# Eight gate tiles moved into the up projection, weights loaded a load ahead at the start, and a written ScalarE order at the end

## The chip, the cores and the metric

One core of a Trainium2 chip runs the whole kernel. Its engines work beside each other, each through its own list of instructions in order: TensorE (PE) multiplies, VectorE (DVE) and ScalarE (ACT) work element by element, GpSimd (POOL) issues some transfers, SyncE (SP) issues most of them. An instruction that waits holds up all that stand behind it on its engine, and a transfer issued from ScalarE stands in ScalarE's list. The metric is the device time of one execution in microseconds: 2152.03 us before, the median of three runs (2150.7 to 2157.48).

## The reference

One layer of a diffusion block over 512 latent tokens and 256 context tokens, width 2048, in float32:

```python
mod_l = (silu(c) @ w_ada + b_ada)          # 6 x 2048 values: sh_a sc_a gt_a sh_f sc_f gt_f
mod_c = (silu(c_ctx) @ w_ada + b_ada)      # the same for the context
h_l = modulate(rms_norm(x, g_mix_norm), sh_a, sc_a)
h_c = modulate(rms_norm(ctx, g_mix_norm), csh_a, csc_a)
...  = split_projection(h_l @ w_in)        # attention of 8 heads, and a gated short convolution
x = x + gt_a * merge_heads(att_l, conv_l, g_mix_out, w_out)
hf_l = modulate(rms_norm(x, g_ffn_norm), sh_f, sc_f)
x = x + gt_f * conv_ffn(hf_l, w_up, ffn_conv_w, ffn_conv_b, w_down)
return rms_norm(x, g_final)
```

## The kernel before

The tokens lie along the free dimension, 512 columns; the width is cut into 16 tiles of 128 rows. Every float32 operand is split into a high part, which ScalarE casts (names that end in h), and a low part, which VectorE subtracts (names that end in l), and a product is three matmuls (`mm3`): high by high, high by low, low by high. So every weight tile needs a transfer, a cast and a subtraction before TensorE can use it.

The work goes through stages, one after the other. **Start**: c and c_ctx are spread over the partitions by matmuls with a row of ones and pass through silu (`silu_rows`, L405 and L406) into sv and svc; the 16 tiles of x are squared on ScalarE and added up on VectorE into one total (`add_squares`, L346, L347), whose column sums (`rms_steps`, L308), square root and reciprocal (`rsqrt`, L281, L283) give the factor rl (L319). **Input projection**: 31 output tiles, the 16 tiles of the width taken in three chunks of 2, 4 and 10. In a chunk the first G = 6 outputs (banks pf) take the tiles as they get ready; then the others follow (banks pp). A tile gets ready by `prep`: its shift and scale are dots of two rows of w_ada with sv on VectorE (two of 128x1024 a tile, L233), then x * rl (L427), scale and shift on ScalarE (L430), and the split into h0h, h0l and so on. Weights are loaded where they are used (`load`, names rf, rw). In the chunk's end `evac` copies a bank on ScalarE (chunk 0, L531) or adds it on VectorE. **Attention**, **output projection**, and in these the late w_ada tiles 32 to 87, two dots of 128x1024 each (`late_dot`, L255). In the last two outputs of the output projection the residual (L955), its squares, the second norm and the modulated tiles hf0, hf1, ... follow each other, and the **up projection** starts on them with the weights ufw0, ufw1, ... (`split4`, L998, L999). From f = 3 on it works by a Strassen-like scheme, seven products of eight triples of matmuls for each f (`product`; p1, p2, p6, q5, p7, and for the f before, q4 and q3), each with a cast of 128x1024 on ScalarE and a subtraction on VectorE. The last eight tiles of w_ada, 88 to 95, are dotted in the **down projection** in quarters of 128x512 (aq, L1249), which works by products of seven triples (v0 to v23; `seven`, `into`). **End**: the two last steps v22 and v23 run interleaved; the final norm is made for each half of the tokens, and the outputs, scaled ahead by g_final on ScalarE (`scale_out`, L1416), are multiplied by the norm's factor (`final`, L1409) and stored.

A planner orders each engine's instructions by its own estimate of durations, except where the code fixes the order: `keep` holds instructions of one engine in the order in which they are written, and `issue_after` puts one behind another. Tiles come from pools: a tile with one buffer can be loaded anew only when its last reader is done.

## Time and profile before

| | us |
|---|---|
| median of three runs | 2152.03 |
| profiled execution | 2158.83 |
| its span, first to last instruction | 2157.0 |
| TensorE busy | 2104.9 |
| VectorE busy | 1769.0 |
| ScalarE busy | 1047.1 |
| first matmul of the input projection | 29.62 |
| first matmul of the up projection | 815.16 |

A line of a timeline has the start and duration of an instruction, its engine and line, what it writes and reads, how many like it follow, and in brackets the time that the engine was idle before it and what it waited for. Where an engine is late the brackets name its releaser, and the releaser's own row tells why that was late. The mean granted clock of TensorE is 0.994 of full speed.

### The profile page before, as it was taken

The page shows a single profiled execution, that of the slowest core. Times are in us where ns is not written, and L with a number is a line of the kernel's source. Part 1 is how long each engine was busy: PE and PEld are TensorE (multiplying, and loading weights), DVE is VectorE, ACT ScalarE, POOL GpSimd, SP SyncE. Part 2 cuts the span into 40 slices and gives each one's busy share as a digit, 9 for nine tenths or more (in the row PEclk, how much of TensorE's full clock was granted, in tenths as well). Part 3 has the DMA queues.
Part 4 walks back from the last instruction along what each step waited for, and adds up shares of the span by engine and source line. Part 5 has one row for each costly group of instructions (what it writes and reads, how often), then busy time and mean ns, then how long its engine had stood idle before and what let it go on. Part 6 is the DMA issues. An engine that isn't in the chain of part 4 may idle for free.

```text
span 2157.0 us, 37744 instructions
## 1 busy us (share of the span) xinstructions
PE 2104.9 (98%) x14458; PEld 1946.7 (90%) x14458; DVE 1769.0 (82%) x2859; ACT 1047.1 (49%) x1710; POOL 188.1 (9%) x270
## 2 busy tenths in 40 slices
PE   7899999999999999999999999999999999999997
PEld 4688788888888888999999999999999889999997
DVE  7998987778886889788888788788888658888877
ACT  5533333555552237555555555555555333333445
POOL 0000000000000000111211111111111000000000
PEclk9999999999999999999999999999999999999998
DMA  9979785334559986577887877877887999877683
GB/s 335 345 275 337 270 279 176 128 126 162 177 199 348 344 278 192 159 217 201 241 232 215 240 229 220 237 231 219 241 229 218 341 335 290 254 220 236 196 247 111
DMA packets 162121, 513.89 MB, mean 238 GB/s; under 512 B 18962, under 2 KB 23314, under 8 KB 156306
## 3 DMA queue, kind: packets, MB, share of 16 engines
q1 hardware_dynamic: 133364, 418.14, 56.5%
q0 software_dynamic: 27488, 92.29, 18.3%
q8 instruction: 113, 1.85, 0.3%
q10 hardware_dynamic: 1088, 1.05, 0.1%
q14 instruction: 68, 0.56, 0.1%
HBM read 464.22 MB, written 46.14 MB: 237 GB/s over the span
## 4 chain that ended last, share of the span: by engine, by line
PE 86%; DVE 6%; DMA 5%; issue 1%; ACT 1%; SPq 0%; DVEq 0%; POOLq 0%; ACTq 0%
PE pp L187 4%; PE pp L189 4%; PE pp L188 4%; PE o L189 1%; PE o L187 1%; PE o L188 1%; DMA ada<-in_w_ada 1%; PE d L187 1%; PE d L189 1%; PE d L188 1%; PE uf L187 1%; PE uf L188 1%; PE of L187 1%; PE of L188 1%; PE of L189 1%
## 5 line engine op out<-in xcount | busy, mean ns | idle before, releaser
L1044 POOL DMA_DIRECT2D t_d<-tp x126 | 71.9, 574 | 468.3 <-DVE tp L1043 465.4
L255 DVE SCALAR_TENSOR_TENSOR ada<-ada,sv 128x1024 f32<-128x1024 f32 x68 | 82.1, 1219 | 12.1 <-DMA ada<-in_w_ada 12.0
L166 ACT CAST w_0h<-rw 128x512 fp32r<-128x512 f32 (+1 forms) x63 | 38.3, 618 | 108.3 <-PE pp L188 63.1
L1121 POOL DMA_DIRECT2D u_s<-in_w_up x80 | 70.2, 878 | 224.4 <-DMA u_s<-in_w_up 131.5
L233 DVE SCALAR_TENSOR_TENSOR ada<-ada,sv 128x1024 f32<-128x1024 f32 x64 | 77.5, 1217 | 4.4 <-DMA ada<-in_w_ada 3.9
L522 DVE SCALAR_TENSOR_TENSOR ada<-ada,svc 128x1024 f32<-128x1024 f32 x64 | 76.0, 1220 | 2.3 <-DMA ada<-in_w_ada 2.3
L785 POOL TENSOR_TENSOR gr<-gr,half 128x8 f32<-128x8 f32 x4 | 10.1, 2524 | 628.7 <-DVE gr L784 536.8
L1042 ACT CAST tp<-a 128x256 fp32r<-128x256 f32 x90 | 34.7, 405 | 60.5 <-DMA t_d<-tp 54.1
L167 DVE TENSOR_TENSOR w_0l<-rw,w_0h 128x512 fp32r<-128x512 f32 (+1 forms) x63 | 42.6, 681 | 22.3 <-ACT w_0h L166 22.3
L255 DVE SCALAR_TENSOR_TENSOR ra<-ra,sv 128x1024 f32<-128x1024 f32 x44 | 52.5, 1217 | 1.1 <-DMA ra<-in_w_ada 1.1
L1213 DVE TENSOR_TENSOR u<-u,u_s 128x1024 f32<-128x1024 f32 x40 | 48.8, 1219 | 0.7 <-DMA u_s<-in_w_up 0.7
L1214 DVE TENSOR_TENSOR u<-u,u 128x1024 f32<-128x1024 f32 x40 | 48.7, 1218 | 0.0
L1043 DVE TENSOR_TENSOR tp<-a,tp 128x256 fp32r<-128x256 f32 x90 | 36.2, 418 | 12.3 <-ACT tp L1042 12.3
L756 ACT CAST pth<-t 128x384 fp32r<-128x384 f32 x64 | 28.6, 485 | 26.4 <-PE t L753 26.4
L1042 ACT CAST tp<-ts 128x256 fp32r<-128x256 f32 x36 | 14.6, 407 | 43.5 <-DMA t_d<-tp 41.1
L533 DVE TENSOR_TENSOR acc<-acc,pp 128x512 f32<-128x512 f32 x50 | 34.0, 680 | 2.1 <-PE pp L189 2.1
L757 DVE TENSOR_TENSOR ptl<-t,pth 128x384 fp32r<-128x384 f32 x64 | 33.2, 549 | 2.7 <-ACT pth L756 2.7
L737 DVE TENSOR_REDUCE mn<-s 128x1 f32<-128x768 f32 x32 | 30.4, 952 | 4.8 <-PE s L726 4.6
L1043 DVE TENSOR_TENSOR tp<-ts,tp 128x256 fp32r<-128x256 f32 x36 | 15.2, 421 | 23.3 <-ACT tp L1042 23.3
L1005 ACT ACTIVATE g<-cg,sm 128x512 f32<-128x512 f32 x40 | 32.5, 813 | 0.5 <-DVE cg L1182 0.5
L1005 ACT ACTIVATE a<-ca,sm 128x512 f32<-128x512 f32 x40 | 32.1, 803 | 0.0
L1013 ACT ACTIVATE g<-g 128x512 f32<-128x512 f32 x43 | 27.2, 632 | 6.4 <-DVE g L1007 6.4
(15967 smaller groups left out, 9398.2 us busy)
## 6 DMA issues: line engine op xcount, KB each, us to landing
ada<-in_w_ada SPq DMA_DIRECT2D x196, 512.0 KB, 6.0
u<-in_w_up SPq DMA_DIRECT2D x120, 512.0 KB, 8.2
w<-t_d SPq DMA_DIRECT2D x161, 256.0 KB, 5.2
u_s<-in_w_up SPq DMA_DIRECT2D x80, 512.0 KB, 4.3
u_s<-in_w_up POOLq DMA_DIRECT2D x80, 512.0 KB, 8.9
t_d<-tp POOLq DMA_DIRECT2D x126, 256.0 KB, 4.9
v<-in_w_dnw SPq DMA_DIRECT2D x72, 384.0 KB, 5.4
ra<-in_w_ada SPq DMA_DIRECT2D x22, 1024.0 KB, 4.9
```

What stands on the lines that cost most here:

```text
L187: PE.matmul(ps, w[0], x[0], start=first, stop=False, skip_group_check=on_top)
L188: PE.matmul(ps, w[0], x[1], start=False, stop=False, skip_group_check=on_top)
L189: PE.matmul(ps, w[1], x[0], start=False, stop=last, skip_group_check=on_top)
L233: V.scalar_tensor_tensor(out=r, in0=r, scalar=1.0, in1=vec[:, i * 1024:(i + 1) * 1024], op0=ALU.mult, op1=ALU.mult, accum_out=col[:, i:i + 1])
L255: keep(V.scalar_tensor_tensor(out=r, in0=r, scalar=1.0, in1=svs[i], op0=ALU.mult, op1=ALU.mult, accum_out=lc[:, t % 4:t % 4 + 1] if i else ...
L522: keep(V.scalar_tensor_tensor(out=raw[q], in0=raw[q], scalar=1.0, in1=svc[:, q * 1024:(q + 1) * 1024], op0=ALU.mult, op1=ALU.mult, accum_o ...
L1005: A.activation(u, src, AF.Identity, bias=s("fb", m), scale=s("fw", 86 + m))
L1042: A.copy(out=z[:, :256], in_=src)
L1043: V.tensor_tensor(out=z[:, 256:], in0=src, in1=z[:, :256].bitcast(F32), op=ALU.subtract)
L1044: G_.dma_start(t_d[p, OPS.index(n)], z.bitcast(F32))
L1121: G_.dma_start(r[-1], src[more], accum_op=ALU.add)
L1213: V.tensor_tensor(out=a11, in0=a11, in1=s1, op=ALU.add)
```

## The change

There are three edits, at the start, from the output projection to the up projection, and at the end.

**Start.** The squares are added into two totals of eight tiles, and both are given to the column sums. c_ctx is no longer spread by matmuls: after chunk 1's first banks it is loaded to all partitions at once, with one silu over 128x2048. The dots of tiles 16 and 0 get places of their own around the reciprocal (`first_scale`, `prep_first`). The input projection's weights are loaded one load ahead (`load_next`, `weights`), and for a while casts and subtractions of weights are put behind the last cast or subtraction of a tile.

**Gate tiles.** The late tiles end at 80. Tiles 80 to 87 are dotted in the up projection, in 32 quarters of 128x512, one transfer from ScalarE each and all in one buffer (tag ts, which `pair_sums` uses too), and four loads of a quarter of sv into rl. A product can issue a quarter or dot the one that is under way, where no background work stands.

**End.** In the last two steps ScalarE's casts, squares and scalings keep the order in which they are written, the scalings of outputs are spread over the products, the weights of the last four products are split early (`apart`), the factor is read from PSUM, and two of the stores of the second half go out from ScalarE instead of four.

```diff
-    late = {"t": 32, "raw": None, "end": 88}
+    late = {"t": 32, "raw": None, "end": 80}
...
-        recips[:] = [V.reciprocal(r, r)]
+        with tc.issue_after(ahead.pop()) if ahead else ExitStack():
+            recips[:] = [V.reciprocal(r, r)]
...
+        def first_scale():
+
+            first["raw"] = [ada_load(t) for t in (16, 0)]
+            first["col"] = [tiny(2, f"dv{t}") for t in (16, 0)]
+            for i in range(2):
+                first["last"] = first_dot(0, i)
+            total(first["col"][0], 16, mod[:, 16:17])
...
+        def prep_first():
+
+            a = first_dot(1, 0, recips[0].ins)
+            with tc.issue_after(a):
+                b = V.tensor_tensor(out=xs[0], in0=xs[0], in1=rl, op=ALU.mult).ins
+            first_dot(1, 1, b)
+            low_after[:] = [total(first["col"][1], 0, mod[:, 0:1]).ins]
...
-            ssq = add_squares(ssq, xs[j], T, f"xs{j}")
-        silu_rows(c_ctx, svc, "cc")
+            ssq = add_squares(ssq if j % 8 else None, xs[j], T, f"xs{j}")
+            if j % 8 == 7:
+                sqs.append(ssq)
         fetch_to(sm, small)
-        rms([ssq], D, T, rl)
+        first_scale()
+        ahead.append(first["last"])
+        rms(sqs, D, T, rl)
...
+        def load_next():
+            if loads:
+                a, k = loads.popleft()
+                ready.append(load(w_in[:, a:a + k], k, f"rw{a}"))
+
+        def weights(ahead=True):
+
+            raw = ready.popleft()
+            if ahead:
+                load_next()
+            return raw
...
-                    prep(q)
+                    prep(q) if q else prep_first()
+                    if q:
+                        load_next()
...
             if ci == 1:
+
+                fetch_to(svc, c_ctx.to_broadcast([P, D]))
+                A.activation(svc, svc, AF.Silu)
...
-                    k = min(per, len(ORDER) - G - i) * n
-                    raw = load(w_in[:, off:off + k * P], k * P, f"rw{ci}_{m}")
-                    off += k * P
+                    raw = weights()
...
+    def gate_mods():
+
+        if way:
+            r, q, i, n = way.pop()
+            if n < 3 and not bg:
+                way.append((r, q, i, n + 1))
+                return
+            V.scalar_tensor_tensor(out=r, in0=r, scalar=1.0, in1=rl, op0=ALU.mult, op1=ALU.mult, accum_out=lu[:, i, q:q + 1])
...
+        elif quarters and not bg:
+            q, i = quarters.popleft()
+            if i == 0:
+                A.dma_start(rl, sv_d[:, q * T:(q + 1) * T])
+            r = cp.tile([P, T], F32, tag="ts", bufs=1, name=f"au{i}{q}")
+            A.dma_start(r, w_ada[80 + i][:, q * T:(q + 1) * T])
+            way.append((r, q, i, 0))
+
     def product(ps, a, n, nm, first):
...
+        gate_mods()
         pump(1)
...
+    def apart(a, nm):
+
+        r = []
+        for c in range(0, WIN * P, T):
+            k = min(T, WIN * P - c)
+            hi, lo = (t2([P, T], F32R, f"{nm}{c}{x}") for x in "hl")
+            keep(A.copy(out=hi[:, :k], in_=a[:, c:c + k]))
...
-            (A if h and j % 4 else SP).dma_start(out[j:j + 2, :, HS[h]].rearrange("a p t -> p a t"), o)
+            (A if h and j % 4 and j > 8 else SP).dma_start(out[j:j + 2, :, HS[h]].rearrange("a p t -> p a t"), o)
...
     d_p6(za)
+    scale(0, [0])
     d_q3(prev)
     ended(prev)
     d_p6(zb)
+    scale(0, [2, 4])
     for z in (za, zb):
         squares(z.m, H0)
     d_p7(za)
+    scale(0, [6, 8])
     d_p7(zb)
+    scale(0, [10])
+    scale(1, [0])
     d_q4(za)
+    za.s1 = apart(za.s1, "xa5")
+    scale(1, [2])
+    d_q4(zb)
     sqs = [ssq, add_squares(None, acc2[za.m + 1][:, H0], T // 2, "eqa", a=0)]
-    scaled = {j: scale_out(j, 0) for j in range(0, za.m, 2)}
-    d_q4(zb)
+    keep(opened[-1])
+    zb.s1 = apart(zb.s1, "xb5")
+    za.a12 = apart(za.a12, "xa3")
+    zb.a12 = apart(zb.a12, "xb3")
+
+    keep(A.activation(tiny(1, "root"), eps, AF.Sqrt))
     sqs.append(add_squares(None, acc2[zb.m + 1][:, H0], T // 2, "eqb", a=0))
...
```

On SP's queue, at the weights of the first chunk (rw is a load of w_in, ada a half of a row tile of w_ada), the order before was:

```order
L145 DMA rw_13_337<-in_w_in 128x2048
L145 DMA ada_360<-in_w_ada 128x1024
L145 DMA ada_362<-in_w_ada 128x1024
L145 DMA ada_368<-in_w_ada 128x1024
L145 DMA ada_370<-in_w_ada 128x1024
L145 DMA ada_449<-in_w_ada 128x1024
L145 DMA ada_451<-in_w_ada 128x1024
L145 DMA ada_457<-in_w_ada 128x1024
L145 DMA ada_459<-in_w_ada 128x1024
L145 DMA rw_21_473<-in_w_in 128x2048
```

and is now:

```order
L145 DMA ada_284<-in_w_ada 128x1024
L145 DMA rw_298<-in_w_in 128x2048
L145 DMA rw_330<-in_w_in 128x2048
L145 DMA ada_353<-in_w_ada 128x1024
L145 DMA ada_355<-in_w_ada 128x1024
L145 DMA ada_361<-in_w_ada 128x1024
L145 DMA ada_363<-in_w_ada 128x1024
L145 DMA ada_442<-in_w_ada 128x1024
```

The load rw_21_473, now rw_330, has moved to right behind the load before it.

On ScalarE, at the end of the first part of the up projection and the first Strassen-like product (T and hf are casts of the operands, ufw and u3p of weights), the order before was:

```order
L998 CAST ufw14h<-ufr_8286 128x768
L1085 CAST T23h<-x_7165 128x256
L1085 CAST T43h<-x_7165 128x256
L941 CAST hf15h<-x_7267 128x512
L998 CAST ufw15h<-ufr_8348 128x768
L1085 CAST hf12h<-x_7071 128x256
L998 CAST u3p1h<-u_11_8242 128x1024
L1085 CAST T23h<-x_7267 128x256
L1085 CAST T43h<-x_7267 128x256
L998 CAST u3p2h<-u_12_8244 128x1024
```

and is now, with au for the quarters of w_ada:

```order
L1266 DMA au_8689<-in_w_ada 128x512
L1163 CAST T23h<-x_7155 128x256
L1163 CAST T43h<-x_7155 128x256
L1073 CAST ufw15h<-ufr_8289 128x768
L1163 CAST hf12h<-x_7065 128x256
L1266 DMA au_8949<-in_w_ada 128x512
L1012 CAST hf15h<-x_7239 128x512
L1266 DMA au_9103<-in_w_ada 128x512
L1163 CAST T23h<-x_7239 128x256
L1073 CAST u3p1h<-u_11_8183 128x1024
L1163 CAST T43h<-x_7239 128x256
L1266 DMA au_9347<-in_w_ada 128x512
```

Four of the first eight quarter loads have come between the casts, each of which waits for VectorE's dot of the one before.

On ScalarE, around the cast v23p6h in the last two steps (out is a scaled output, eq a square for the final norm, both of sums c), the order before was:

```order
L1416 ACTIVATE out_23626<-c_19120,sm 128x256
L1416 ACTIVATE out_23626<-c_19122,sm 128x256
L1416 ACTIVATE out_23629<-c_19124,sm 128x256
L1416 ACTIVATE out_23629<-c_19126,sm 128x256
L1416 ACTIVATE out_23728<-c_18797,sm 128x256
L1416 ACTIVATE out_23728<-c_18799,sm 128x256
L1416 ACTIVATE out_23731<-c_18801,sm 128x256
L1416 ACTIVATE out_23731<-c_18803,sm 128x256
L1416 ACTIVATE out_23734<-c_18805,sm 128x256
L1416 ACTIVATE out_23734<-c_18807,sm 128x256
L1416 ACTIVATE out_23737<-c_18809,sm 128x256
L998 CAST v23p6h<-v_23322 128x768
```

and is now:

```order
L1073 CAST v21q3h<-v_22974 128x768
L359 ACTIVATE eq_23555<-c_19168 128x512
L359 ACTIVATE eq_23558<-c_19170 128x512
L1073 CAST v23p6h<-v_23366 128x768
L1534 ACTIVATE out_23584<-c_18845,sm 128x256
L1534 ACTIVATE out_23584<-c_18847,sm 128x256
L1534 ACTIVATE out_23587<-c_18849,sm 128x256
L1534 ACTIVATE out_23587<-c_18851,sm 128x256
L359 ACTIVATE eq_23590<-c_19172 128x256
L359 ACTIVATE eq_23593<-c_19176 128x256
L1073 CAST v22p7h<-v22s_23172 128x768
```

The eleven scalings ahead of v23p6h have gone, and two squares have come there; scalings follow behind it.

## Rows read from the trace of the kernel before

**Rows 1.** The page, busy time of each engine, share and instructions

```profile
PE 2104.9 (98%) x14458; PEld 1946.7 (90%) x14458; DVE 1769.0 (82%) x2859; ACT 1047.1 (49%) x1710; POOL 188.1 (9%) x270
```

**Rows 2.** Stretches: busy us (instructions) by engine, granted clock, DMA share, GB/s

```profile
30.00:100.00 70.00, 60.98 (x246) 46.34 (x246) 62.72 (x126) 38.10 (x70) 0.00 (x0) 1.00 0.92 340
862.00:900.00 38.00, 38.00 (x228) 33.74 (x227) 29.14 (x46) 20.74 (x33) 2.83 (x4) 1.00 0.52 139
900.00:1650.00 750.00, 750.00 (x6252) 750.00 (x6252) 621.63 (x823) 429.95 (x644) 133.96 (x199) 1.00 0.80 226
815.00:820.00 5.00, 4.83 (x29) 4.84 (x30) 5.00 (x13) 4.96 (x13) 0.00 (x0) 0.67 1.01 397
```

**Rows 3.** TensorE's waits: us in total, times, longest

```profile
PE pp L187 <- ACT acc L531: 7.2, 6, 2.0
```

**Rows 4.** Timeline at the start: start, us, engine, instruction, [idle before <- releaser]

```profile
22.75 1.87 PE L308 MATMUL rs<-io,xs0t 128*128 128x1 f32 x8
29.62 2.07 PE L187 MATMUL pf<-h0h,wf_0h 128*128 128x512 f32 x4 [3.21 <-ACT h0h L329]
...
18.80 0.69 DVE L347 TENSOR_TENSOR xs0t<-xs0t,xs 128x512 f32<-128x512 f32 x1
19.41 1.22 DVE L233 SCALAR_TENSOR_TENSOR ada<-ada,sv 128x1024 f32<-128x1024 f32 x1
...
25.06 0.18 DVE L283 RECIPROCAL rr<-rr 128x4 f32<-128x4 f32 x1 [0.41 <-ACT rr L281]
```

**Rows 5.** Timeline in the first chunk, ScalarE and TensorE

```profile
53.31 0.62 ACT L166 CAST w_0h<-rw 128x512 fp32r<-128x512 f32 x1 [6.04 <-DMA rw<-in_w_in]
...
54.46 0.50 PE L187 MATMUL pp<-h0h,w_0h 128*128 128x512 f32 x1 [1.98 <-ACT acc L531]
...
57.73 0.50 PE L187 MATMUL pp<-h0h,w_0h 128*128 128x512 f32 x1 [1.62 <-ACT acc L531]
```

**Rows 6.** Timeline at the step into the up projection

```profile
814.28 0.83 ACT L998 CAST ufw0h<-ufr 128x768 fp32r<-128x768 f32 x1
...
809.73 0.28 PE L189 MATMUL ol<-mx15h,o151w1536l 128*128 128x256 f32 x1
...
815.16 0.58 PE L187 MATMUL uf<-hf0h,ufw0h 128*128 128x256 f32 x1 [0.88 <-ACT ufw0h L998]
```

**Rows 7.** Line L1249 by groups; landing of aq's loads, then of rq's

```profile
L1249 DVE SCALAR_TENSOR_TENSOR aq<-aq,svq 128x512 f32<-128x512 f32 x32 | 21.2, 687 | 7.7 <-DMA aq<-in_w_ada 6.1 <-DMA svq<-sv_d 1.7
...
DMA to landing us min/median/max: 3.0/6.0/8.3
...
DMA to landing us min/median/max: 2.5/2.7/3.4
```

**Rows 8.** Tiles u14p6l and u3p6l: xcount, ns min/median/max, first and last start

```profile
L189 PE MATMUL u14a<-T20h,u14p6l x2: 285/285/285, 1112.2 to 1112.6; 128*128 128x256 f32 x2
...
L999 DVE TENSOR_TENSOR u14p6l<-u,u14p6h x1: 1226/1226/1226, 1107.4 to 1107.4; 128x1024 fp32r<-128x1024 f32 x1
...
L189 PE MATMUL u3a<-T20h,u3p6l x2: 284/284/284, 890.7 to 891.1; 128*128 128x256 f32 x2
```

**Rows 9.** Timeline at the end: ScalarE, VectorE, TensorE

```profile
2115.25 4.50 ACT L1416 ACTIVATE out<-c,sm 128x256 f32<-128x256 f32 x11
2119.66 0.82 ACT L998 CAST v23p6h<-v 128x768 fp32r<-128x768 f32 x1
...
2128.11 1.28 ACT L1467 ACT_TABLE_LOAD   x1
2129.40 0.20 ACT L1467 ACTIVATE root<-eps 128x1 f32<-128x1 f32 x1
...
2118.90 0.48 DVE L1338 SCALAR_TENSOR_TENSOR c<-v21c,mod,c 128x256 f32<-128x256 f32 x1 [1.65 <-PE v21c L189]
...
2120.53 0.38 PE L187 MATMUL v23a<-w,v23p6h 128*128 128x256 f32 x1 [1.67 <-ACT v23p6h L998]
...
2137.08 0.50 PE L308 MATMUL rs<-io,eqbt 128*128 128x1 f32 x4
```

More of the change, by code (lines that the diff above doesn't have):

```diff
@@ L426, in modulate @@
             xr = xs[j]
[L427 removed]
+            if j:
+                keep(V.tensor_tensor(out=xr, in0=xr, in1=rl, op=ALU.mult))
             sc = tiny(1, f"sc{j}")
@@ L554, in block_kernel @@
         todo[1, 22] = [(prep, 13)]
-        off = 0
+        loads, off = deque(), 0
+        for n in KCH:
+            per = max(1, 2048 // (n * P))
+            for k in [2 * G] * (n // 2) + [min(per, len(ORDER) - G - i) * n for i in range(0, len(ORDER) - G, per)]:
+                loads.append((off, k * P))
+                off += k * P
+        ready = deque()
+        def load_next():
[8 more added lines that the diff above has]
+        load_next()
         for ci, (k0, n) in enumerate(zip(K0, KCH)):
@@ L1228, in block_kernel @@
     finish(pend)
+    assert not quarters and not way
     phc.close()
@@ L1444, in block_kernel, with scale @@
     za, zb = nxt, weights_of(STEPS - 1)
+    written[0] = True
+    scaled = {}, {}
+    def scale(h, js):
+        for j in js:
+            scaled[h][j] = scale_out(j, h)
     d_p1(za)
@@ L1456, in block_kernel, with factor @@
     d_p7(za)
+    scale(0, [6, 8])
     d_p7(zb)
+    scale(0, [10])
+    scale(1, [0])
     d_q4(za)
+    za.s1 = apart(za.s1, "xa5")
+    scale(1, [2])
+    d_q4(zb)
     sqs = [ssq, add_squares(None, acc2[za.m + 1][:, H0], T // 2, "eqa", a=0)]
[L1460 to L1467 removed]
+    keep(opened[-1])
[3 more added lines that the diff above has]
+    keep(A.activation(tiny(1, "root"), eps, AF.Sqrt))
+    sqs.append(add_squares(None, acc2[zb.m + 1][:, H0], T // 2, "eqb", a=0))
+    fac = []
+    def factor(steps):
+        for r in steps:
+            fac.append(r)
+            yield
+    bg.append(factor(rms_steps(sqs, D, 0, T // 2, None, wait=1, one=True, hold=True)))
+    outs = final(0, fac, scaled[0])
     pump(1)
@@ L1470, in block_kernel @@
     squares(za.m + 1, H1)
-    d_q5(zb, (1,), lambda: [keep(next(outs)) for _ in range(2)])
+    d_q5(zb, (0,), lambda: [keep(next(outs)) for _ in range(2)])
     keep(last_into[0])
+    scale(0, [12, 14])
     squares(zb.m + 1, H1)
-    scaled = {j: scale_out(j, 1) for j in range(0, za.m, 2)}
     keep(next(outs))
@@ L1490, in block_kernel @@
         keep(ins)
-    for ins in final(1, r, scaled):
+    scale(1, [8, 10, 12, 14])
+    for ins in final(1, r, scaled[1]):
         keep(ins)
```

78 lines of the change are left out of this document (56 added, 22 removed).

## The prediction

> **What bounds the kernel now.** I read the busy times first. The reader is to see that TensorE is busy for 2104.9 of 2157.0 us [rows 1], so at most about 52 us can be had without taking matmuls away, and the change takes none. Next came the table by stretches: where TensorE is busy all the time, as in nearly the whole up projection [rows 2] (third row), nothing is to be won, and something can be lost. Between 30 and 100 us it is idle for 70.00 − 60.98 = 9.02 us [rows 2] (first row). Then I read TensorE's waits [rows 3] and, at each place that the change touches, the timeline of the engines that TensorE waits for: the start [rows 4, 5], the step into the up projection [rows 6] and the end [rows 9]. The profiled execution took 2158.83 us, 1.83 us of it outside its span, and the median of the runs shown is 2152.03 us; I sum changes of the span and take them off the median.
>
> **The start.** Before, TensorE runs the eight matmuls that spread c and c_ctx until 22.75 and only then sums the squares [rows 4]. The c_ctx half, and the four ScalarE steps behind it, leave the start. In the changed order the last square's addition is one fewer (0.69 us off DVE's chain, which ended at 18.80 + 0.69 = 19.5), so the sums can run from 18.7, in 1.87 us, to 20.6; the table load (1.28 us, as in [rows 9]) fits in while ScalarE waits, and the square root is ready near 20.9. Two dots of 1.22 us stand on DVE before the reciprocal, 18.7 to 21.0, so the reciprocal comes near 21.1 (25.06 before). From there the old chain has 29.62 − 25.06 = 4.56 us to the first matmul; the new one has a second dot behind the multiply (1.22 us) but no weight lows ahead of it, and I put it at 5.5 us: first matmul 26.6, **−3.0 us**.
>
> **The first chunk.** Two of the six waits for the copy out of a bank, 1.98 and 1.62 us [rows 5], have one cause: ScalarE, in its order, stood 6.04 us at a cast for a weight load and the copies stood behind it. That load (rw_21 before, rw_330 now) stands right behind the load before it on SP's queue, ahead of the eight ada loads that stood between, so I take both away: **−3.6**. The four other waits make 7.2 − 3.6 = 3.6 us [rows 3]. They come from ScalarE's in-order wait for VectorE at xr, and VectorE is some 3 to 4 us earlier now; I take half, **−1.8** (bounds 0 and −3.6). Against it: the three matmuls that filled the wait for h1h now stand behind it, 3 x 0.25 us (60.98 us for 246 matmuls, the first row of [rows 2]), **+0.7**; and the weight loads now go ahead of ada loads for which VectorE waits. Their cost the trace does not show; it is between 0 and the 3.6 us that comes free, and I take **+1.5**. Context's silu moves behind chunk 1's first banks: one load, one long activation and a table load on ScalarE, where no row of TensorE's waits stands between 90 and 200 us, and two casts are made ahead of it, which hide it; uncovered it would cost its table load, 1.3 us, and about 2 us of activation. I take 0. Start and first chunk: −3.0 − 3.6 − 1.8 + 0.7 + 1.5 = **−6.2** (−10 to −3).
>
> **The step into the up projection.** VectorE has the dots of the last late tiles between the residuals there; the first matmul of the up projection starts 815.16 − 810.0 = 5.2 us after the last of the output projection [rows 6]. With eight tiles gone, no dot stands there. The last residual can follow the last matmul at about 810.3; behind it on ScalarE now stand one square, one scaled tile and the cast ufw0h, of which the cast is the longest with 0.83 us; I put the three at 1.8 us, so the first matmul comes near 812.1: **−3.0**. Behind the gap the granted clock was 0.67, between its two levels of 1.2 and 2.4 GHz (0.5 and 1), for 4.83 busy us [rows 2] (fourth row), which cost about 1.6 us; if a shorter gap spares that, it is −4.6; the other end is −2.
>
> **The price in the up projection.** The 16 dots of 1.22 us become 32 of 0.69 us [rows 7], 22 us of VectorE, each with its own load of 256 KB. All go through one buffer: each load waits, on ScalarE's queue, for the dot before it, and the casts queued behind it wait as well. Eight stand close together at the start, two in each odd f after that, 12 such pairs. Where landing takes as long as the same size took at its best-served place, 2.7 us median, the casts and lows of u3 come in time by my count and TensorE loses nothing; at 6.0, the median of the later gate's loads [rows 7], the eighth link of the chain brings u3p6l by my count at 896.2 against 890.7 where it is wanted [rows 8]: 5.5 us. Between them the cost begins at about 3.2 us of landing. The DMA engines are half busy in that stretch, 0.52 [rows 2] (second row), so I lean to the first row: **+1.5** (0 to 5.5). In the pairs, VectorE's lows are done 1112.2 − 1108.6 = 3.6 us before TensorE wants them [rows 8], and a pair's second load is issued about 3.0 us before its dot: a landing up to 6.6 us costs nothing, so I take 0 there. The Trainium skill ("DMA: Bandwidth & Descriptors", Anatomy of one DMA) gives about 2 us and the bytes at 436 GB/s, by which 256 KB would be an estimated 2.6 us; the 2.7 row agrees, the 6.0 row does not, and by the page the sum would be 1.5 us lower. The same page (Issuing engines are not separate DMA queues) speaks against the change: a load from ScalarE's queue shares the 16 engines with the up projection's stream; by that the 6.0 row is nearer, and the sum would be 4.0 us higher. Which of the two holds no row tells, since nothing was loaded from ScalarE's queue there.
>
> **The end.** Before, TensorE waits 1.67 us at v23p6h, because eleven output scalings stood before that cast on ScalarE (2115.25 to 2119.66) [rows 9]. The change takes them away from there but writes two squares ahead of the cast, and these need the sum that VectorE makes at 2118.90 to 2119.38. So: squares at 2119.42 and 2119.95, cast 2120.47 to 2121.30, first matmul 2121.3 instead of 2120.53: **+0.8**. The early weight pieces for the last four products cost ScalarE and VectorE work that lies beside matmuls. Six short casts, the table load and the root then stand before the square eqbt, on which the first half's sum waits: 2138.4 by my count against 2137.08 [rows 9], of which 0.8 is counted; **+0.5**. The outputs behind the second reciprocal remain eight of 0.6 us, and the stores behind them the same bytes: 0. The end: **+1.3** (−1 to +3). In the trace the table load took 1.28 us and the root began 1.29 us after its start [rows 9]. The Trainium skill ("ScalarE: Activation LUTs", What ACT_TABLE_LOAD costs) adds a drain of about 1.38 us to each load; the row shows none, and by the page the end would be 1.4 us later still.
>
> **Sum.** −6.2 − 3.0 + 1.5 + 1.3 = −6.4 us: a span of 2150.6, a profiled execution of 2152.4, and against the median 2152.03 − 6.4 = **2145.6 us**. What a measurement can tell from no change is 0.3%, 6.5 us, so my value lies on that border.
>
> **Rivals.**
> (1) All stalls go: the first chunk's other half (−1.8), no contention there (−1.5), no price in the up projection (−1.5), and no slow clock after the shorter gap (−1.6): −6.4 − 6.4 = −12.8, 2139.2 us. For it: VectorE is idle for 7 us between 30 and 100 and is the last cause of most waits. Against: the DMA engines are full there (0.92) [rows 2], so something arrives late.
> (2) The chain of eight loads becomes the wait that ends last: 5.5 in place of 1.5, −2.4, 2149.6 us. For it: the same loads' median of 6.0; against: DMA engines half idle in that stretch, and 2.7 us for the same size elsewhere [rows 7].
> (3) Slower: the second load of each pair decides. VectorE stands in order at that dot with u..p6l behind it. At 8.3 us, the longest of the same loads [rows 7], it stands 8.3 − 3.0 = 5.3 us, 1.7 more than the 3.6 us of cover; 12 pairs cost 20 us, with (2) 20 − 2.4 = +17.6, 2169.6 us; at 7.6 us it is 1.0 a pair, 12 − 2.4 = +9.6, 2161.6 us. It decides from a landing of 6.6 us up. For it: the DMA engines carry the weights and the products' stores all through that stage, 0.80 busy [rows 2]. Against: the dots can fall behind and catch up, for VectorE is busy for only 621.63 of 750 us there [rows 2].
> (4) The change does not do what it says at the end: if the two squares are not what ScalarE stands at, the 1.67 us wait goes and the end is −1.2 instead of +1.3: 2143.1 us, inside the main case.
>
> **How the numbers follow.** Main case, with (4), 0.48: 2142 to 2149. Rival (1) 0.20: 2138 to 2142. Rival (2) 0.20: 2148 to 2151. Rival (3) 0.12: 2154 to 2170. The range from 2138 to 2154 leaves out (3) and a little below. Faster means under 2145.6: just over half of the main case and all of (1), 0.46. Slower means over 2158.5: most of (3), 0.10. Within: 0.44.
>
> **What would show it.** Right: the first pf matmul near 26.6, no wait for the copies near 54 and 58, the first uf matmul 2 to 2.5 us after the last residual's matmul, au loads landing in 3 us or less at the start of the up projection, TensorE busy without a gap through all its pairs, and a wait of over 2 us at v23p6h. Wrong: gaps of 1 us and more repeated at the p6 products (rival 3), a gap of some 5 us at u3 or u4 (rival 2), VectorE waiting for ada loads in the first chunk longer than before, or a v23p6h that starts before 2120 less the time won.

## The result, and the profile after

The changed kernel takes 2161.42 us, the median of nine executions (2151.39 to 2166.44); the kernel before, run beside it, takes 2151.78 (2148.32 to 2157.71). The ratio is 1.0039, with a 95% interval of 1.0023 to 1.0055. It is slower, with an interval that stays clear of 1. The forecast was 2145.6 us with a range to 2154: wrong in sign and out of range.

The profiled execution of the change took 2151.39 us, 10 below its own median, while that of before, 2158.83, lies 7 above its. A comparison of those two spans alone would show a gain of 7.4 us that the medians turn round. So stages are compared below, and with more than one execution.

The busy time of the engines, from the page of the change, answers to [rows 1]:

```profile
PE 2090.8 (97%) x14458; PEld 1935.2 (90%) x14458; DVE 1766.0 (82%) x2893; ACT 1047.4 (49%) x1712; POOL 188.1 (9%) x270
```

The same stretches as in [rows 2], the second moved 7 us and the last to its place behind the step: stretch, length, busy us (instructions) of PE, PEld, DVE, ACT, POOL, granted clock, DMA share, GB/s.

```profile
30.00:100.00 70.00, 63.28 (x255) 48.99 (x254) 60.41 (x121) 40.33 (x70) 0.00 (x0) 0.98 0.91 336
855.00:893.00 38.00, 36.50 (x214) 31.90 (x214) 30.32 (x54) 19.52 (x31) 2.26 (x3) 1.00 0.62 168
900.00:1650.00 750.00, 744.56 (x6246) 742.09 (x6245) 631.16 (x873) 427.16 (x642) 134.80 (x200) 1.00 0.82 236
808.00:815.00 7.00, 6.70 (x57) 6.70 (x57) 6.58 (x13) 5.41 (x13) 0.00 (x0) 1.00 0.94 325
```

The third row is the one that matters: where TensorE was busy for 750.00 of 750 us [rows 2], it now has holes. The fourth row has a clock of 1.00 where it was 0.67. The first has 0.98 where it was 1.00; what that is follows below.

The start, TensorE and VectorE, answers to [rows 4]:

```profile
18.67 1.87 PE L316 MATMUL rs<-io,xs8t 128*128 128x1 f32 x8 [4.01 <-DVE xs8t L360]
26.87 2.07 PE L193 MATMUL pf<-h0h,wf_0h 128*128 128x512 f32 x4 [4.64 <-ACT h0h L337]
...
20.88 0.18 DVE L291 RECIPROCAL rr<-rr 128x4 f32<-128x4 f32 x1
22.88 0.69 DVE L448 TENSOR_TENSOR xr<-xr,rl 128x512 f32<-128x512 f32 x1 [0.50 <-ACT rl L327]
```

In the first chunk TensorE still waits five times for a copy out of a bank. These are three of the five in its timeline, and the cast on ScalarE ahead of the longest; they answer to [rows 5]:

```profile
55.43 0.50 PE L193 MATMUL pp<-h0h,w_0h 128*128 128x512 f32 x1 [0.96 <-ACT acc L571]
...
68.83 0.50 PE L193 MATMUL pp<-h0h,w_0h 128*128 128x512 f32 x1 [0.95 <-ACT acc L571]
72.56 0.55 PE L193 MATMUL pp<-h0h,w_0h 128*128 128x512 f32 x1 [2.08 <-ACT acc L571]
...
71.40 0.62 ACT L167 CAST wf_0h<-rw 128x512 fp32r<-128x512 f32 x1 [1.39 <-DMA rw<-in_w_in]
```

TensorE at the step into the up projection, against [rows 6]: 2.7 us from the last matmul of the output projection to the first uf, where it was 5.2.

```profile
805.35 0.28 PE L195 MATMUL ol<-mx15h,o151w1536l 128*128 128x256 f32 x1
807.35 0.61 PE L316 MATMUL rs<-io,fq0t 128*128 128x1 f32 x4 [1.72 <-DVE fq0t L360]
808.30 0.39 PE L193 MATMUL uf<-hf0h,ufw0h 128*128 128x256 f32 x1 [0.34 <-ACT ufw0h L1073]
```

TensorE's waits between 870 and 1670 us (in all, times, longest), three of eight, which make 6.8 us. Before, it had none there.

```profile
PE u22b L195 <- DVE u22p2l L1077: 1.6, 1, 1.6
PE u25a L195 <- DVE u25p6l L1077: 1.1, 1, 1.1
PE u3a L195 <- DVE u3p6l L1077: 1.0, 1, 1.0
```

To see why u22p2l is late, follow the timeline back, TensorE first, then VectorE and ScalarE:

```profile
1257.85 0.39 PE L195 MATMUL u22b<-hf1h,u22p2l 128*128 128x256 f32 x1 [1.56 <-DVE u22p2l L1077]
...
1254.83 1.23 DVE L1318 TENSOR_TENSOR u<-u,u_s 128x1024 f32<-128x1024 f32 x1 [3.46 <-DMA u_s<-in_w_up]
1256.58 1.22 DVE L1077 TENSOR_TENSOR u22p2l<-u,u22p2h 128x1024 fp32r<-128x1024 f32 x1
...
1266.10 0.41 ACT L1120 CAST tp<-ts 128x256 fp32r<-128x256 f32 x1 [4.26 <-DMA t_d<-tp]
1275.86 0.41 ACT L1120 CAST tp<-a 128x256 fp32r<-128x256 f32 x1 [3.55 <-DMA t_d<-tp]
```

VectorE's low u22p2l stands behind a sum of weights (u) that waited 3.46 us for u_s, which SyncE loads and GpSimd then adds to. GpSimd issues the stores t_d too, and a cast tp waits for such a store to free its buffer; the two casts shown stand behind u22p2l and ahead of the next late low, u23p2l. In all, VectorE and ScalarE wait so in the change, from their waits:

```profile
DVE au L1255 <- DMA au<-in_w_ada: 21.1, 21, 2.3
DVE u L1318 <- DMA u_s<-in_w_up: 16.7, 11, 3.5
...
ACT tp L1120 <- DMA t_d<-tp: 145.9, 68, 4.6
```

and ScalarE before:

```profile
ACT tp L1042 <- DMA t_d<-tp: 93.0, 61, 2.9
```

The second row of the change has no counterpart among VectorE's waits of before. The quarters' loads landed after (shortest, median, longest; first all 32, then the 24 in pairs behind 900 us), to be held against [rows 7]:

```profile
DMA to landing us min/median/max: 3.0/4.9/10.2
...
DMA to landing us min/median/max: 3.4/8.4/10.2
```

The median of all hides two groups. Of each pair the first load, issued late in an even f, landed after 8.4 to 10.2 us, the second, in the odd f behind it, after 3.4 to 4.9 (where the trace has the landing).

The end, ScalarE, then TensorE, answers to [rows 9]:

```profile
2110.11 1.15 ACT L359 ACTIVATE eq<-c 128x512 f32<-128x512 f32 x2 [5.97 <-DVE c L1455]
2111.16 0.82 ACT L1073 CAST v23p6h<-v 128x768 fp32r<-128x768 f32 x1
...
2127.47 1.28 ACT L1598 ACT_TABLE_LOAD   x1
2128.76 0.20 ACT L1598 ACTIVATE root<-eps 128x1 f32<-128x1 f32 x1
...
2112.03 0.39 PE L193 MATMUL v23a<-w,v23p6h 128*128 128x256 f32 x1 [2.48 <-ACT v23p6h L1073]
```

The squares eq stand 5.97 us for VectorE's sum c, and the cast behind them makes TensorE wait 2.48 us, where it was 1.67.

### The profile page after: what moved, and what is told of

Its sections match the earlier page's. It is cut to its first block, busy times and chain, and to the rows that moved or that the text cites. A ratio compares the mean times of both kernels' runs of the same rounds, so it can differ in the third digit from the quotient of the medians.

```text
span 2149.6 us, 37791 instructions
## 1 busy us (share of the span) xinstructions
PE 2090.8 (97%) x14458; PEld 1935.2 (90%) x14458; DVE 1766.0 (82%) x2893; ACT 1047.4 (49%) x1712; POOL 188.1 (9%) x270
## 5 line engine op out<-in xcount | busy, mean ns | idle before, releaser
L240 DVE SCALAR_TENSOR_TENSOR ada<-ada,sv 128x1024 f32<-128x1024 f32 x60 | 72.8, 1227 | 2.5 <-DMA ada<-in_w_ada 2.4
L262 DVE SCALAR_TENSOR_TENSOR ada<-ada,sv 128x1024 f32<-128x1024 f32 x52 | 62.9, 1224 | 13.1 <-DMA ada<-in_w_ada 13.1
L1318 DVE TENSOR_TENSOR u<-u,u_s 128x1024 f32<-128x1024 f32 x40 | 48.9, 1222 | 16.7 <-DMA u_s<-in_w_up 16.7
L1255 DVE SCALAR_TENSOR_TENSOR au<-au,rl 128x512 f32<-128x512 f32 x32 | 22.1, 691 | 21.2 <-DMA au<-in_w_ada 21.1
L1083 ACT ACTIVATE g<-cg,sm 128x512 f32<-128x512 f32 x40 | 32.6, 815 | 6.3 <-DVE cg L1287 5.9
```

The costliest lines, as they stand in the source:

```text
L240: V.scalar_tensor_tensor(out=r, in0=r, scalar=1.0, in1=vec[:, i * 1024:(i + 1) * 1024], op0=ALU.mult, op1=ALU.mult, accum_out=col[:, i:i + 1])
L262: keep(V.scalar_tensor_tensor(out=r, in0=r, scalar=1.0, in1=svs[i], op0=ALU.mult, op1=ALU.mult, accum_out=lc[:, t % 4:t % 4 + 1] if i else ...
L1083: A.activation(u, src, AF.Identity, bias=s("fb", m), scale=s("fw", 86 + m))
L1318: V.tensor_tensor(out=a11, in0=a11, in1=s1, op=ALU.add)
```

## The experiments

The executions of one kernel spread over 10 us and more, and part of this is clock: before, those under 2147 us had a mean granted clock of 0.995 to 0.997, those over 2157 one of 0.992 to 0.995. So each kernel has a second number here: the mean, over its executions, of time times mean granted clock, an estimate of what it would take at full clock. For before this came out between 2140.9 and 2142.2 us in five sessions. The last column is the difference to before in the same session (for the change, to 2141.2, near which four of the five lie). Each difference is uncertain by some 2 us (two standard errors). The product also gives back low clock under which TensorE had nothing to do, such as the 0.50 of the change's last 8 us, behind its last matmul; so it is a rough number.

| kernel | runs | median us | ratio, 95% interval | mean clock | at full clock |
|---|---|---|---|---|---|
| before, one session | 33 | 2151.56 | | 0.9948 | |
| the change | 9 | 2161.42 | 1.0039 (1.0023–1.0055) | 0.9939 | +5.5 |
| start alone (e2) | 12 | 2151.83 | 0.9992 (0.9978–1.0007) | 0.9945 | −2.3 |
| end alone (e3) | 10 | 2156.17 | 1.0028 (1.0016–1.0040) | 0.9939 | +2.8 |
| start and gate tiles (e4) | 12 | 2156.02 | 1.0021 (1.0005–1.0036) | 0.9946 | +3.1 |
| without the gate tiles (e1) | 12 | 2158.76 | 1.0031 (1.0014–1.0047) | 0.9922 | −0.5 |
| end, casts first (e9) | 12 | 2156.02 | 1.0012 (0.9999–1.0026) | 0.9939 | +2.0 |
| end, sums later (f2) | 12 | 2155.35 | 1.0006 (0.9992–1.0021) | 0.9937 | −0.3 |
| end, both casts clear (g1) | 12 | 2151.72 | 0.9996 (0.9981–1.0011) | 0.9953 | −0.2 |
| start, and that end (g3) | 12 | 2150.12 | 0.9986 (0.9973–0.9998) | 0.9948 | −2.3 |

At full clock the three parts add up: −2.3 for the start, 3.1 + 2.3 = +5.4 for the gate tiles, +2.8 for the end, together +5.9 against +5.5 measured. The other 2 us of the change are clock: 0.9939 against 0.9948 of some 2150 us. In mean times, without any correction, they add up as well: −1.7 for the start, +3.5 + 1.7 = +5.2 for the gate tiles, +4.6 for the end, together +8.1 against +7.3 for the change, each uncertain by 2 to 3 us. That the sums agree to less than this is partly luck.

**Without the gate tiles (e1).** The late tiles end at 88 again, and `product` makes no quarters.

```diff
-    late = {"t": 32, "raw": None, "end": 80}
+    late = {"t": 32, "raw": None, "end": 88}
...
-        gate_mods()
```

> The start and the end as changed, but the gate tiles 80 to 87 back as late tiles in the output projection, so no quarter work in the up projection. Theory 1 (the quarters in the up projection cost 10 to 15 us that the change gives elsewhere back): about 2149 us, the median of before less 4 at the start and plus 1 at the end; TensorE busy 750 of 750 us in the up projection. Theory 2 (the start or the end is what became slower in the timed runs): 2160 us or so, like the change, spread over 15 us.

Measured: 2158.76 us, as slow as the change to within the intervals, though TensorE has no hole left in the up projection:

```profile
900.00:1650.00 750.00, 750.00 (x6253) 750.00 (x6252) 620.58 (x822) 428.88 (x642) 133.62 (x199) 1.00 0.79 226
```

By its time alone (+6.1 us in the mean) the gate tiles would nearly be acquitted. The last column says otherwise: it runs at −0.5, and what it loses counts there as clock. Its trace shows where the two cancel: from chunk 3's first matmul (h6h) to u3's first it takes 719.6 us, 9.7 more than the change and 5.0 more than before, so it loses at the step what it wins in the up projection. There it shows the low clock that the change is spared (same columns; TensorE had been busy for 1.30 of the 5 us ahead):

```profile
810.00:815.00 5.00, 2.83 (x11) 2.35 (x12) 4.42 (x18) 4.12 (x10) 0.00 (x0) 0.50 0.97 360
815.00:820.00 5.00, 5.00 (x30) 5.00 (x29) 4.45 (x9) 4.63 (x11) 0.00 (x0) 0.61 0.96 362
```

That accounts for a few us of one trace; the mean clock of its executions, 0.9922, is a little lower than that trace's 0.993, and where the rest went was not followed up. So the whole without one part measures that part together with what it spares elsewhere, and the parts were run alone.

**The parts (e2, e3, e4), and before once more.** Each takes over one or two of the three groups of edits.

> The kernel before with the edits of the start alone. In the profiles of the change and of the run without quarters, chunk 1 starts 3.9 and some 3 us earlier. Theory 2a (the start gives what it shows, the price is elsewhere): about 2149 us, 3 to 4 below before. Theory 2b (the start's new order of loads or casts costs more later than it gives, by waits that come and go between executions): 2153 us or more.

> The kernel before with the edits of the end alone. Theory 2a, if the end holds the price: about 2157 us, 5 above before or more, with a wait of 2.5 us at v23p6h where before has 1.7. Theory 2b: 2153 to 2154 us, the 1.3 us that the prediction gave the end.

> The change without the edits of the end: the start and the quarters in the up projection. If the end holds the price: about 2153 us (2161 less 8). If the start or the quarters hold it: 2158 to 2161 us.

> The kernel before once more, for a second trace of it. Its times are those of before, 2152 us within 3. If the executions of one kernel differ by waits at the last products of the down projection (v19 to v22, where the trace of before shows three of about 0.9 us and that of the change one), this trace shows another number of them, and its time goes with that number. If they differ elsewhere, the starts of v0 and v22 lie as far apart as in the first trace.

Measured: the table; before again 1.0006 (0.9994–1.0018). The start wins little, the end loses, the gate tiles lose; start and gate tiles together (2156.02) fall between their two theories, so each part holds a share. Before's second trace has one wait at v19 to v22 where the first had four, and takes 328.3 us from v0 to v22 where the first took 331.5. Where the gate tiles lose is read from the first matmuls of u3 and of u42 (line, count, durations, first and last start): in before, in the change's profiled execution, and in another of its executions, which took 2157.77 us.

```profile
L187 PE MATMUL u3a<-hf0h,u3p1h x1: 288/288/288, 884.5 to 884.5; 128*128 128x256 f32 x1
L187 PE MATMUL u42a<-hf0h,u42p1h x1: 281/281/281, 1662.1 to 1662.1; 128*128 128x256 f32 x1
```

```profile
L193 PE MATMUL u3a<-hf0h,u3p1h x1: 287/287/287, 876.2 to 876.2; 128*128 128x256 f32 x1
L193 PE MATMUL u42a<-hf0h,u42p1h x1: 280/280/280, 1656.5 to 1656.5; 128*128 128x256 f32 x1
```

```profile
L193 PE MATMUL u3a<-hf0h,u3p1h x1: 288/288/288, 876.9 to 876.9; 128*128 128x256 f32 x1
L193 PE MATMUL u42a<-hf0h,u42p1h x1: 280/280/280, 1665.1 to 1665.1; 128*128 128x256 f32 x1
```

From u3 to u42 before took 777.6 us, and so did nine other traces without quarters (f3's took 775.4). The change took 780.3 and 788.2.

**The change three times more (one execution each).**

> The change once more, for a second trace. Its first trace fell on an execution of 2151 us, 10 below its median. Theory 3 (the price is the quarters in the up projection, which come and go): in an execution of 2158 us and more, the stretch from u10 to u42 is 5 us and more longer than before's 645 us, by waits of TensorE for p2 and p6 lows. Theory 4 (the price is the end): from v22 to the end 5 us and more longer than before's 55 us.

Measured: 2150.33, 2159.37 and 2157.77 us. From u10 to u42 they took 645.4, 650.1 and 654.3 us (before 645.2), from v22 to the end 56.6, 58.4 and 55.2: theory 3. From u3 to u42 it was 781.1, 786.5 and 788.2 us. With the profiled execution of the result (2151.39 us and 780.3) the order is clear: the two executions of 2150 and 2151 us pay 2.7 to 3.5 us there, the two of 2158 and 2159 pay 8.9 to 10.6.

These figures are net of something that the waits bring with them. TensorE, busy all the time at a granted clock of 1.00, has two paces: before, one f takes 20.16 us (from its first matmul to the next one's), in most of the change 19.94. The same two stand in f3's trace (below; no quarters), which waits once, for 0.6 us at u27. Two stretches of 80 us, ahead of u27 and behind it:

```profile
1040.00:1120.00 80.00, 80.00 (x669) 80.00 (x668) 65.98 (x90) 45.88 (x69) 14.72 (x22) 1.00 0.80 229
1560.00:1640.00 80.00, 80.00 (x676) 80.00 (x675) 66.76 (x90) 46.33 (x70) 14.98 (x23) 1.00 0.80 231
```

Before has 669 matmuls in both stretches, the profiled execution of the change 676 in the second. Over 36 f the quicker pace is worth up to 8 us, so the waits in the change cost more than the 2.7 to 10.6 us that are left. The execution of 2159.37 us kept the slow pace up to u14; in that of 2157.77 the clock falls once more, to 0.66 in 1490 to 1495.

**Quarters in another buffer (e5), loads without dots (e7), dots without loads (e8).** The first gives the quarter a tile of the pool for temporaries instead of the one that the pair sums use; the second leaves out the dots, the third the loads (its dots read sv alone).

```diff
-            r = cp.tile([P, T], F32, tag="ts", bufs=1, name=f"au{i}{q}")
+            r = tmp([P, T], F32, f"au{i}{q}")
```

> The change with the quarters loaded into the pool of five temporary tiles in place of the one buffer that the pair sums share. If the one buffer is the price (a load that waits for the dot before it, the pair sums that wait for the dot, casts behind both): 2145 to 2152 us and the waits for au under half of 21 us. If the landing time itself or the traffic is: 2158 to 2163 us, the waits for au about 21 us.

> The change with the 32 dots left out; the 32 loads stay in ScalarE's list and in their one buffer, so the gate's tiles 80 to 87 are only the bias. Theory 1a splits: if VectorE standing at the dot is the price, 2143 to 2148 us; if the traffic of 8 MB beside the weights and the stores is the price, about 2160 us. Theory 1b: 2143 to 2148 us.

> The change with the 32 quarter loads of w_ada left out; the 32 dots stay, in the same places, and read a row of sv that is there, so the gate's scale is not the model's. Theory 1a (the wait for the quarter loads, on VectorE and in ScalarE's list, is the price): 2143 to 2148 us, no gap in the up projection. Theory 1b (VectorE's 22 us of dots are the price): about 2161 us, like the change.

Measured: ratios of 1.0359 (1.0334–1.0384), 1.0083 (1.0063–1.0102) and 1.0224 (1.0201–1.0247): every one slower than the change, and outside all their theories. The loads without dots still cost 8.5 us between u3 and u42 (786.1 us), all of it behind u10, so a price of this size in the pairs does not need the 22 us of dots on VectorE; ahead of u3 this kernel loses another 10 us, at the step (719.7 us from h6h to u3, 709.9 in the change). The other two tell of something else. Their longest waits in the up projection are for the first cast of a product, as here in the kernel without loads,

```profile
PE u37a L193 <- ACT u37p1h L1073: 2.5, 1, 2.5
PE u19a L193 <- ACT u19p1h L1073: 2.5, 1, 2.5
```

since the planner there put a cast tp, which waits for a store, right before u..p1h on ScalarE. They changed the order as well as the resource, and their times say nothing of the buffer. Two things can be read from the traces all the same. In seven traces with all 32 loads the stores t_d land after 5.5 to 5.9 us in the median, in the eleven without quarters after 4.8 to 5.2, with dots and no loads after 5.1: the stores are late where the loads are, not where only the dots are. And ten casts tp wait for a pair sum ts in the change, 10.3 us in all, none before and none with the quarters in another buffer, which points to the shared buffer.

**One quarter per pair (f4).** Five tiles instead of eight in the up projection, one quarter for each odd f after the first eight, and the end as before. The gate that this kernel makes is not the model's.

```diff
-    quarters = deque((q, i) for q in range(4) for i in range(8))
+    quarters = deque((q, i) for q in range(4) for i in range(5))
...
-        elif quarters and not bg:
+        elif quarters and not bg and not held[0]:
```

> The start's edits and quarters, with one quarter in each odd f in place of two: 20 quarters (five tiles), the other three tiles late as before. If the second load of a pair is the price: u10 to u42 645 to 646 us as before, and 2150 to 2153 us (2156 with pairs). If each load costs alike: u10 to u42 647 us and more, and 2154 us or more.

Measured: 1.0268 (1.0246–1.0291), and ScalarE's timeline at u13 shows the same order again:

```profile
1078.83 0.40 ACT L1112 CAST tp<-a 128x256 fp32r<-128x256 f32 x1 [4.79 <-DMA t_d<-tp]
1079.14 1.04 ACT L1068 CAST u13p1h<-u 128x1024 fp32r<-128x1024 f32 x1
```

So it cannot tell whether the second load of a pair is the cause. What it shows is that a waiting cast in ScalarE's order, just ahead of u..p1h, costs far more than the loads. Whether the price needs the loads in ScalarE's list at all, or only their 8 MB, stays untested: no kernel loaded the quarters from another queue.

**Earlier dots without moving tiles (f1).** To have the step's gain without quarters, the start alone with the late dots made more often (`often=m > 4` in place of `m > 9`).

> The start's edits alone, and all late tiles to 87 dotted earlier in the output projection (three tiles in each of its outputs in place of two in most), so that none stands at the step into the up projection, and no quarters. If the step's gain of 4.7 us comes from the missing dots alone: the first matmul of the up projection 4 us earlier than in the run of the start only, u3 to u42 777.6 us as before, and 2145 to 2148 us. If the output projection cannot carry them (transfers 0.89 busy there): waits for weights between 630 and 800 us, and 2151 us or more.

Measured: 1.0039 (1.0024–1.0055). TensorE waits at the last output but one of the output projection:

```profile
PE ol L193 <- ACT o150w0h L167: 12.9, 1, 12.9
...
630.00:800.00 170.00, 157.05 (x703) 128.29 (x702) 137.02 (x253) 43.42 (x74) 10.89 (x16) 0.97 0.93 334
```

In SyncE's order the loads of w_ada had come ahead of that output's weights. Transfers are busy for 0.93 of the stretch; in before 0.90, in the change 0.82. In this order, at least, the gain at the step cannot be had with the 8 MB of the eight tiles left in this stretch; an order that keeps that output's weights ahead was not tried.

**The end's written order (e9, f2, g1).** First the two squares behind the cast v23p6h, then also the column sums behind v22q4's matmuls, then the squares behind v22p7h as well.

```diff
-    ended(prev)
     d_p6(zb)
     scale(0, [2, 4])
+    d_p7(za)
+    ended(prev)
     for z in (za, zb):
         squares(z.m, H0)
-    d_p7(za)
...
+    sum_after[:] = last_mm
```

> The end's edits alone, as in the run of the end only, with the two squares of v21's sums written behind the cast v23p6h. Theory 4 (the squares hold up the cast, and this with what follows is the end's price of 4.6 us): no wait at v23p6h, and 2150 to 2153 us. Rival (the early casts and the table load ahead of eqbt, or the stores, are the price): still 2155 us or more, with a wait of over 1 us at the first half's sum.

> The end's edits alone, with the two squares behind the cast v23p6h as in the run before and TensorE's first sum of squares held behind v22q4, where before had it. If these two places are the end's price: no wait over 0.6 us at v23p6h or the sum, v22 to the end 52 to 54.5 us in the trace (55 in before's, 57 with the edit), and 2150 to 2153 us. If something else of the edit is: still 2155 to 2157 us.

> The end of the change alone, with the first two squares written behind the casts v23p6h and v22p7h, and the column sums of the squares held behind the matmuls of v22q4. Theory (the price of the end is ScalarE's written order: whatever is written behind the two squares inherits their wait for VectorE, and moving them only moves the wait): with nothing that TensorE wants soon written behind them, no wait of TensorE over 0.6 us at v23p6h, at the sum or at v22p7h, and the stretch from the first matmul of v22 to the end at or under 54.5 us, where the change has about 57; the time is within 0.2% of before, 2149 to 2154 us. Rival (the price is the early weight pieces and the spread scalings, work that the order adds anywhere): no wait at the squares, yet the stretch stays at 56 to 57 us, and the time 2154 to 2158 us.

Measured, the longest waits of TensorE behind 2060 us, first of e9, then of f2, then of g1:

```profile
PE rs L308 <- DVE ssq L350: 2.8, 1, 2.8
```

```profile
PE v22a L188 <- ACT v22p7h L1005: 2.8, 1, 2.8
```

```profile
PE rs L310 <- ACT eqbt L348: 0.7, 1, 0.7
PE v23a L188 <- ACT v23p7h L1005: 0.7, 1, 0.7
```

By their times e9 and f2 came out as their rivals said, since each had only moved the wait: from the cast to the sums, from there to the next cast. Only when nothing that TensorE wants soon stood behind the squares did it go, but for 0.7 us twice, one of them at the sum, where g1's theory allowed 0.6. From the first matmul of v22 to the end g1 takes 51.9 us and g3, with the same end, 53.9; the kernels with the end of the change take 55.2 to 58.8, before 55.3, the other kernels with before's end 53.6 to 54.9. The scalings spread over the products and the early pieces of weights are in all of them, so no cost of theirs shows.

The waits also show in the clock. From the first matmul of v22 to the last matmul, before, e3, f2 and g1 (length, busy us, clock third from the end):

```profile
2101.70:2147.10 45.40, 40.57 (x317) 39.21 (x316) 34.32 (x56) 31.07 (x63) 0.85 (x1) 0.96 0.27 83
2098.80:2146.70 47.90, 41.57 (x317) 40.29 (x316) 34.68 (x60) 28.18 (x60) 0.85 (x1) 0.93 0.25 76
2099.00:2147.60 48.60, 43.05 (x317) 41.76 (x316) 35.08 (x60) 28.47 (x60) 0.85 (x1) 0.89 0.25 77
2097.90:2139.90 42.00, 38.58 (x317) 37.60 (x316) 34.54 (x60) 28.31 (x60) 0.85 (x1) 1.00 0.27 80
```

**The start, with early dots and f2's end (f3), and with g1's end (g3).**

> The start's edits, the early dots of f1 and the mended end of f2 together. If both mends hold: 2143 to 2147 us, under before and the change. If they don't: 2150 us or more.

> The start of the change with that end, the late tiles where they were before (88 of them ahead of the up projection). Theory (the start saves some 4 us of span by the first uf matmul and the end costs nothing once its squares stand clear): first matmul of chunk 3's first banks h6h near 165 to 166, up projection busy 750 of 750 us, the stretch from v22 to the end at or under 54.5 us; 2146 to 2151 us, a ratio under 0.999. Rival (what the start wins is given back by the slow clock at the step into the up projection, as in the start alone): 2151 to 2154 us, a ratio of 0.999 to 1.001.

Measured: f3 1.0046 (1.0029–1.0063), with f1's wait of 12.8 us; g3 0.9986 (0.9973–0.9998), 2150.12 us against 2152.91. It is the one version of the study whose interval lies below 1, by less than the 0.3% that the prediction takes as the least to be told from no change.

## Why the prediction was wrong

The forecast was −6.4 us and the medians differ by +9.6. Three terms share the miss. In mean times the start alone gave −1.7 us where its two terms made −6.2; the gate tiles +5.2 where the step and the price in the up projection made −3.0 + 1.5 = −1.5; the end +4.6 where +1.3 stood. The mechanism failed in the second; the other two were in the main mis-sized.

**The start** was right in its first rows: first pf matmul 26.87 against 26.6 forecast; the square sums at 18.67 against 18.7, the reciprocal at 20.88 against 21.1.

**The first chunk** was half wrong. I took away 3.6 + 1.8 us of waits for copies; 7.2 us in six became 5.7 in five. The two waits near 54 and 58 did shrink, to one of 0.96, but one of 2.08 has come at 72.56, where ScalarE's order holds a cast that waited 1.39 us for its weights, and behind it the clock falls, to 0.79 in 70 to 75 us. From the first pf matmul to chunk 3's first (h6h) before took 140.3 and 139.9 us in two executions, the kernels with the new start 136.9 to 141.3. With the earlier start, h6h came at 164.0 to 168.1 us instead of 169.9 and 168.9, at 166.3 and later only in the three traces with that fall of the clock: some 4 us in the mean, not 6.2. The start alone keeps about 3 of them at u3 (880.5 against 884.5 and 883.2) and 1.7 in its mean time.

**The step** was right in kind and small by the clock: −2.5 us from gap to gap (forecast −3.0), and the clock behind it 1.00 instead of 0.67 [rows 2], which I priced at 1.6 and left out. From h6h to u3's first matmul the change takes 709.9 us, before 714.6, the start alone 715.8: −4.7, the −4.6 of the text. e1 shows the other side: with a gap of 8.0 us the low clock comes back.

**The price in the up projection** is the step that failed. Of the first eight loads I took +1.5: u3p6l makes TensorE wait 1.0 us and from u3 to u10 it loses 0.9 to 3.9 us in the four traces, within the bounds of 0 to 5.5; that held. "In the pairs … a landing up to 6.6 us costs nothing, so I take 0 there" was wrong. It priced the second load of a pair, and those landed in 3.4 to 4.9 us, under the mark, while the first loads, which I had not priced, took 8.4 to 10.2; and the stretch from u3 to u42 lost 2.7 to 10.6 us. I had followed one way only, from the dot to the low u..p6l behind it on VectorE. In the profiled execution VectorE never stood at a dot for more than 2.3 us, and the p6 lows make 2.1 of TensorE's 6.8 us of waits, u..p2l 3.9 (0.7 of 4.8, 3.1 of 6.5 and 5.1 of 9.9 in the three other traces). These come by a longer way. Stores t_d land later, pair sums and casts tp come later on ScalarE, and VectorE's work behind them; SyncE's loads wait for VectorE to leave a weight buffer (67.6 us at tp between 1000 and 1660 us, 51.8 before; at ts 32.6, before none); and VectorE stands 16.7 us at sums that need u_s. Counted from each f's first matmul, in the mean from u11 to u41, SyncE issues the second u_s 1.2 us later than before, GpSimd adds to it 1.1 us later, and the sum starts 1.2 us later: the delay is there at SyncE, and GpSimd adds none. Rival 3 named the place and a sum of the right size (9.6 us and up) but the wrong mechanism, and I gave it 0.12. That the chain runs so is read from the trace. That the stores land late where the loads are, with the dots or without, is shown; that the shared buffer holds up the pair sums is what the waits at ts point to; how much of the price each makes is not shown, since each kernel that moved the one or the other moved the order too.

**The end** was mis-sized: +1.3 forecast. v23p6h waited 2.48 us instead of 1.67 as forecast (+0.8), but I looked at that one cast, and left out the clock that the waits cost. e3 cost 2.8 us at full clock and 4.6 in its median; g1 shows that the places of the squares and of the column sums make it. That TensorE's own column sums had moved forward in its order, from behind v22q4 to before v22p7h, I had not seen.

**Table load and landing.** The table load took 1.28 us and the root began 1.29 us after its start again; the Trainium skill ("ScalarE: Activation LUTs", What ACT_TABLE_LOAD costs) adds a drain of about 1.38 us, which this row does not show either. The quarters landed in 3.0 us at best, 4.9 in the median and 8.4 to 10.2 as the first of a pair; by the Trainium skill ("DMA: Bandwidth & Descriptors", Anatomy of one DMA), which gives its figure for transfers that GpSimd issues, I had estimated 2.6. Another section of the Trainium skill's page ("DMA: Bandwidth & Descriptors", Issuing engines are not separate DMA queues: transfers of all engines run on the same 16 DMA engines) was the better guide: the share of the DMA engines rose from 0.80 to 0.82 in the stretch, and stores t_d landed in 5.7 us in the median where it was 4.9.

**What stays open.** The four traced executions of the change took 2154.7 us in the mean; the eight others of the nine timed runs 2160.9. In the traces the time goes with the price between u3 and u42; whether that holds for the others no trace shows. Waits, pace and clock make up what one execution pays there, 2.7 us or 10.6; what decides between them stays open.

## What to carry to other kernels

Work put beside an engine that is busy all the time is not free because its own deadline holds: follow every queue that it enters to the next thing that each of them issues, and from there to the full engine. A wait in an in-order engine belongs to whatever is written behind it; moving the waiting instruction moves the wait, until nothing wanted soon stands behind it. Try each part alone, and set the clock beside the time, before a part is blamed or cleared.

## What was not expected of the hardware

- TensorE keeps one of two paces while it is busy at a granted clock of 1.00, 1.1% apart: 20.16 or 19.94 us for an f. In ten traces of eleven without quarters it never waited there, kept the slow one, and the stretch took 777.6 us; in f3's it changed at its one wait, of 0.6 us, and the stretch took 775.4. In the down projection a step takes 15.12 or 14.95 us, before the one, in the end alone from v6 on mostly the other. So part of the spread between executions is pace; the rest lies in waits and in the clock. What sets the pace no run shows.
- Short waits cost twice. The end of the change costs 2.8 us at full clock, but its mean granted clock fell from 0.9948 to 0.9939, some 2 us more; f2, with no cost at full clock (−0.3), has 0.9937 and a median 1.5 us above before's. In their traces the clock from v22 to the last matmul was 0.93 and 0.89, before's 0.96, and 1.00 where the waits were gone (g1).
- The quarters landed in 3.0 to 10.2 us, for the same 256 KB from the same queue and at a mean DMA share of 0.82; their place in the work made it, the first of each pair 8.4 to 10.2, the second 3.4 to 4.9.
